# A diffusion layer on one core: the channel mixer in one hand-written order, its down projection in pairs of rows

## The chip, the cores and the metric

The kernel runs on one core of one Trainium2 chip. The metric is device time in microseconds (us) of one execution. The core has five engines that run side by side and wait for each other by semaphores: TensorE (PE; its weight loads are shown as PEld), VectorE (DVE), ScalarE (ACT), GpSimd (POOL) and SyncE (SP), whose queue issues all the data transfers (DMA) of this kernel. Matrix products are written to the eight banks of PSUM; everything else lies in SBUF. Before the change three runs took 1354.81 to 1363.58 us, with a median of 1354.82.

## The reference

One layer of a diffusion backbone: a mixer of mLSTM and attention heads, then a channel mixer, on 1024 latent tokens (and 256 context tokens, which end before the channel mixer), D_MODEL = 1024, D_FF = 2816. Only the channel mixer and the final norm matter here:

```python
def conv_glu(h, w_up, conv_w, conv_b, w_down):
    a, val = jnp.split(h @ w_up, 2, axis=-1)
    a = jax.nn.gelu(dwconv(a, conv_w, conv_b))   # depthwise, width 3, over tokens
    return (a * val) @ w_down
# x = x + gate * conv_glu(modulate(rmsnorm(x, norm_ffn)), ...);  out = rmsnorm(x, final_norm)
```

`h` is 1024 x 1024, `w_up` 1024 x 5632, `w_down` 2816 x 1024, all float32.

## The kernel before, in words

**Products.** Operands are split into a high and a low part (`wh` and `wl`, `hi` and `lo`): ScalarE copies the number to fp32r (a CAST), VectorE subtracts that from the number, and TensorE multiplies high x high, high x low and low x high. A product of one 128-wide weight tile with 512 columns over 4 steps of depth is `prod`: 12 matmuls. Both projections use a scheme in the manner of Strassen and Winograd: seven products of half-size blocks instead of eight, at the price of sums of weights and of results.

**Up projection.** There are 22 blocks, each of 128 gate channels and 128 value channels; they come in the order 0, 11, 1, 12 and so on (`blocks`), as the halves of the rows of `w_down` need them in pairs. The transposed activations `hB` hold seven sums B11, B21, B22 and T1 to T4. For one block the weights (1 MB, four quarters) are loaded into `R` (`load_R`), a tile of seven slots with one buffer. Three slots are sums (`load_up`: two by VectorE, two by GpSimd, one of them in place), and four `wsplit` cut it into `wh` and `wl`: three of 1024 columns, one of 512. The seven products of a block (`upm`) have these names below:

- a = W0[0] x B11, and A = W0[1] x B21, added into the same bank;
- b = W1[1] x T2; c = W1[0] x T1; e = W2[1] x T3; d = W2[0] x T4;
- C = W3 x B22, added into the bank of c.

`sn` is ScalarE's copy of a, made before A. VectorE forms u2 = b + sn, u3 = e + u2, `av` (its second half = c + u3, its first half = d + u3), and after C the value `vt` = c + u2. Then come Identity on ScalarE (`tt` = w av + bias), two taps of the convolution on VectorE, Gelu on ScalarE, the product with a + A on VectorE and that with `vt` on GpSimd. `store` and `combine` put the result, and in every second block its sums with the block before (s1, s2, s4 by GpSimd), into `act_d` in memory; `tt` has two buffers. Block 0 is written out by hand ahead of the loop, up to `fence.__exit__`; behind it only SP's order is written by hand (`sp_order`), and for the other engines a planner decides the order.

**Down projection.** There are seven products m1, m6, m2, m7, m5, m4, m3 of a 512 x 1408 by a 1408 x 512 half each, with 11 rows (`kt`) of 128 each. A step is one row: `load` fetches the row of weights (256 KB) and of activations (256 KB), `cut` splits both, `dprod` does 12 matmuls, 3 into each of the four banks X or Y. `load` runs 6 steps ahead (AHEAD), and steps 1 to 4 are prepared before the last `store` and `combine`. While m1 and m6 run, `sums` makes b22 = b22 - b12 (GpSimd) and b11 = b22 + b11 (VectorE), which m6, m7 and m4 use. Behind each product `after` holds its epilogue for the four tiles, one at a time; behind m4 and m3 stands the final norm (`end2`, `end1`). The last 5 rows (TAIL) of m3 are done tile by tile, so that the norm of one tile runs beside the products of the next.

Of the kernel before, what the change touches and what calls it, by code (L numbers as in the profile page):

```python
# [8 lines left out]
F32 = mybir.dt.float32  # L9
# [8 lines left out]
P = 128  # L18
# [35 lines left out]
DB = 6  # L54
RB = 6
TAIL = 5
AHEAD = 6
# [16 lines left out]
def build(tc, I, out, dbg=None):  # L74
# [1281 lines left out]

    def load_R(m):
        R = fr.tile([P, 7, 512], F32, name="R", tag="R")
        nc.sync.dma_start(R[:, 0:4], I["w_up"][m].rearrange("p q k f -> p q (k f)"))
        return R  # L1360

    def wsplit(R, i, w, eng=V):
        wt = [fw.tile([P, w, 512], F32R, name=f"w{n}{w}", tag=f"w{n}{w}", bufs=5 if w == 2 else 2) for n in "hl"]
        S.copy(wt[0][:], R[:, i:i + w])  # L1364
        sub(eng, wt[1][:], R[:, i:i + w], wt[0][:].bitcast(F32))
        return wt

    def load_up(R):
        add(V, R[:, 4], R[:, 3], R[:, 2])
        sub(V, R[:, 5], R[:, 4], R[:, 0])  # L1370
        sub(G, R[:, 3], R[:, 0], R[:, 3])
        sub(G, R[:, 6], R[:, 1], R[:, 5])
        return [wsplit(R, 0, 2), wsplit(R, 4, 2), wsplit(R, 2, 2), wsplit(R, 6, 1)]
# [3 lines left out]
    add(G, R[:, 4], R[:, 3], R[:, 2])  # L1377
    sub(G, R[:, 5], R[:, 4], R[:, 0])
    sub(G, R[:, 6], R[:, 1], R[:, 5])
# [4 lines left out]
    wB = wsplit(R, 6, 1, V)  # L1384
# [3 lines left out]
    wS = wsplit(R, 4, 2, G)  # L1388
# [14 lines left out]
    sub(G, R[:, 3], R[:, 0], R[:, 3])  # L1403
    sum34(7)
    sum34(4)
    wA = wsplit(R, 2, 2, V)
# [4 lines left out]
    fence.__exit__(None, None, None)  # L1411
# [3 lines left out]

    def upm(m, W, before):
        w = lambda i: spc("ffc", 4 * m + i)
        h1, h2_ = slice(0, 512), slice(512, 1024)
        u2 = fs.tile([P, 512], F32, name="u2", tag="u2")
        u3 = fs.tile([P, 512], F32, name="u3", tag="u3", bufs=1)  # L1420
        av = fs.tile([P, SEQ], F32, name="av", tag="av", bufs=1)
        vt = fs.tile([P, 512], F32, name="vt", tag="vt", bufs=1)
        tt = fs.tile([P, SEQ], F32, name="tt", tag="tt")
        if m == 0:
            a, (c_, b_, f_, e_, d_) = ar0, (ps0[n] for n in "cbfed")
            u2b = fs.tile([P, 512], F32, name="u2b", tag="u2")
            add(V, u2[:], b_[:], ar0[:])
            add(V, ar0[:], ps_a2[:], ar0[:])
            add(V, u2b[:], f_[:], u2[:])
            add(V, u3[:], e_[:], u2[:])  # L1430
            add(V, av[:, h2_], c_[:], u3[:])
            add(V, av[:, h1], d_[:], u3[:])
            add(V, vt[:], c_[:], u2b[:])
        else:
            sn = fs.tile([P, 512], F32, name="sn", tag="sn")
            a = newp(pA, "pa", "a")
            prod(a, W[0], 0, B11, True, True)
            S.copy(sn[:], a[:])
            c_, b_ = newp(pB, "pc", "b"), newp(pB, "pb", "b")
            prod(b_, W[1], 1, T2, True, True)  # L1440
            add(V, u2[:], b_[:], sn[:])
            prod(c_, W[1], 0, T1, True, True)
            e_ = newp(pB, "pe", "b")
            prod(e_, W[2], 1, T3, True, True)
            add(V, u3[:], e_[:], u2[:])
            add(V, av[:, h2_], c_[:], u3[:])
            prod(a, W[0], 1, B21, False, True)
            d_ = newp(pB, "pd", "b")
            prod(d_, W[2], 0, T4, True, True)
            add(V, av[:, h1], d_[:], u3[:])  # L1450
            prod(c_, W[3], 0, B22, False, True)
            add(V, vt[:], c_[:], u2[:])
# [19 lines left out]
        def combine():  # L1472
            if m < KD:
                return
# [292 lines left out]
```

## Time and profile before

| | us |
|---|---|
| three runs: median (lowest, highest) | 1354.82 (1354.81, 1363.58) |
| profiled execution, its own time | 1360.57 |
| its span | 1358.6 |
| block 0 from its first product on | 686.6 to 716.9 |
| block 1 and the last product before block 2 | 716.9 to 743.7 |
| blocks 2 to 21 | 743.7 to 1135.85 |
| down projection | 1135.85 to 1350.4 |
| tail behind the last product | 1350.4 to 1358.6 |

A line of the profile's groups names the source line, engine, operation, and output<-input by the program's names, then shapes, a count, busy time and mean. In brackets stands how long the engine stood idle before, and what ended that. A line of the time order begins with the start in us from the span's start and the duration; a trailing x2 says that two like it follow each other at once. Most splits and sums share a helper's line (L1190, L1355, L1173, L1174), so they are told apart by their tiles. `SPq` rows are issues of transfers.

### The profile page before, as it was taken

The page shows a single profiled execution, that of the slowest core. Times are in us where ns is not written, and L with a number is a line of the kernel's source. Part 1 is how long each engine was busy: PE and PEld are TensorE (multiplying, and loading weights), DVE is VectorE, ACT ScalarE, POOL GpSimd, SP SyncE. Part 2 cuts the span into 40 slices and gives each one's busy share as a digit, 9 for nine tenths or more (in the row PEclk, how much of TensorE's full clock was granted, in tenths as well). Part 3 has the DMA queues.
Part 4 walks back from the last instruction along what each step waited for, and adds up shares of the span by engine and source line. Part 5 has one row for each costly group of instructions (what it writes and reads, how often), then busy time and mean ns, then how long its engine had stood idle before and what let it go on. Part 6 is the DMA issues. An engine that isn't in the chain of part 4 may idle for free.

```text
span 1358.6 us, 20088 instructions
## 1 busy us (share of the span) xinstructions
PE 1281.5 (94%) x7141; PEld 1084.9 (80%) x7141; DVE 980.0 (72%) x1806; ACT 619.3 (46%) x1262; POOL 502.1 (37%) x484
## 2 busy tenths in 40 slices
PE   5999999999898899999978999999999999999997
PEld 4789898999898777778756887778778777787886
DVE  5654787776774788997798666676667675879696
ACT  7532243344464576776754232233323232544454
POOL 0440131313446133332443544454544432455430
PEclk9899899999999899999998999999999999999999
DMA  9431443340025422121422233323332335894745
GB/s 361 158 105 32 141 143 121 107 135 5 19 79 177 156 70 94 63 83 44 157 100 83 76 110 109 100 74 115 116 98 88 117 109 186 269 334 123 250 155 186
DMA packets 83395, 171.43 MB, mean 126 GB/s; under 512 B 12864, under 2 KB 25312, under 8 KB 80480
## 3 DMA queue, kind: packets, MB, share of 16 engines
q1 hardware_dynamic: 83296, 170.16, 38.2%
q8 instruction: 56, 0.92, 0.3%
q14 instruction: 43, 0.35, 0.1%
HBM read 131.84 MB, written 38.29 MB: 125 GB/s over the span
## 4 chain that ended last, share of the span: by engine, by line
DVE 26%; PE 18%; DMA 11%; issue 5%; ACT 5%; POOL 2%; SPq 0%; DVEq 0%; ACTq 0%; POOLq 0%
DMA R<-in_w_up_dram 8%; PE pd L1643 7%; DVE wl L1190 7%; PE u L1070 2%; DVE tt L1454 2%; DVE tt L1455 2%; PE po L298 2%; DVE al L1174 2%; PE po L300 1%; PE po L299 1%; ACT tt L1457 1%; DMA ar<-act_a 1%; DVE nm L1018 1%; DVE dl L1174 1%; DVE hB L1190 1%
## 5 line engine op out<-in xcount | busy, mean ns | idle before, releaser
L1364 ACT CAST wh<-R 128x1024 fp32r<-128x1024 f32 (+1 forms) x87 | 81.4, 940 | 188.6 <-DMA R<-in_w_up_dram 147.2
L1190 POOL TENSOR_TENSOR R<-R 128x512 f32<-128x512 f32 x45 | 86.9, 1939 | 128.1 <-DVE R L1355 127.3
L1190 DVE TENSOR_TENSOR wl<-R,wh 128x1024 fp32r<-128x1024 f32 (+1 forms) x86 | 124.6, 1470 | 5.1 <-ACT wh L1364 5.1
L1283 PE MATMUL pc<-hB,wh 128*128 128x512 f32 x344 | 110.8, 403 | 12.8 <-DVE av L1355 10.8
L1643 PE MATMUL pd<-dh,ah 128*128 128x512 f32 x300 | 116.8, 390 | 1.4 <-ACT ah L1173 1.4
L1643 PE MATMUL pd<-dl,ah 128*128 128x512 f32 x300 | 116.8, 390 | 0.8 <-DVE dl L1174 0.7
L1643 PE MATMUL pd<-dh,al 128*128 128x512 f32 x300 | 116.9, 390 | 0.5 <-DVE al L1174 0.3
L1283 PE MATMUL pa<-hB,wh 128*128 128x512 f32 x336 | 103.8, 389 | 0.0
L1283 PEld LDWEIGHTS pc<-hB,wh 128*128 128x128 f32 x344 | 64.6, 192 | 32.4 <-DVE av L1355 17.0
L1174 DVE TENSOR_TENSOR al<-ar,ah 128x512 fp32r<-128x512 f32 x76 | 71.2, 938 | 19.9 <-ACT ah L1173 19.6
L1355 DVE TENSOR_TENSOR R<-R 128x512 f32<-128x512 f32 x21 | 14.5, 691 | 90.8 <-DMA R<-in_w_up_dram 90.8
L537 PE MATMUL pp<-hl,wh 128*128 128x512 f32 x256 | 79.8, 403 | 0.0
L660 POOL TENSOR_SCALAR dm<-ident,mh 128x128 fp32r<-128x128 f32 x64 | 27.5, 431 | 137.3 <-PE pe L667 96.7
L1173 ACT CAST ah<-ar 128x512 fp32r<-128x512 f32 x76 | 47.1, 620 | 65.1 <-DMA ar<-act_s 33.8
L298 PE MATMUL pv<-wh,hl 128*128 128x256 f32 x256 | 75.7, 296 | 0.0
L1283 PEld LDWEIGHTS pa<-hB,wh 128*128 128x128 f32 x336 | 63.2, 188 | 13.2
L299 PE MATMUL pv<-wl,hl 128*128 128x256 f32 x256 | 73.1, 285 | 0.0
L300 PE MATMUL pv<-wh,hl 128*128 128x256 f32 x256 | 72.9, 285 | 0.0
L1459 POOL TENSOR_TENSOR tt<-vt,tt 128x512 f32<-128x512 f32 x22 | 29.9, 1360 | 111.7 <-ACT tt L1457 74.2
L1283 PE MATMUL pc<-hB,wl 128*128 128x512 f32 x172 | 68.5, 398 | 0.0
L1643 PEld LDWEIGHTS pd<-dh,ah 128*128 128x128 f32 x300 | 56.3, 188 | 13.9 <-ACT ah L1173 2.3
L1643 PEld LDWEIGHTS pd<-dl,ah 128*128 128x128 f32 x300 | 56.3, 188 | 13.4 <-DVE dl L1174 1.7
(1060 smaller groups left out, 4028.0 us busy)
## 6 DMA issues: line engine op xcount, KB each, us to landing
R<-in_w_up_dram SPq DMA_DIRECT2D x22, 1024.0 KB, 6.1
w<-in_w_ada_dram SPq DMA_DIRECT2D x64, 256.0 KB, 2.8
br<-in_w_down_dram SPq DMA_DIRECT2D x55, 256.0 KB, 4.5
ar<-act_s SPq DMA_DIRECT2D x44, 256.0 KB, 3.8
act_a<-tt SPq DMA_DIRECT2D x33, 256.0 KB, 6.7
act_s<-tt SPq DMA_DIRECT2D x33, 256.0 KB, 6.4
ar<-act_a SPq DMA_DIRECT2D x33, 256.0 KB, 4.5
wr<-in_w_h_dram SPq DMA_DIRECT2D x16, 512.0 KB, 5.0
```

The source lines that it names most:

```text
L298: T.matmul(ps, st_hi, mv_hi, start=first, stop=False)
L299: T.matmul(ps, st_hi, mv_lo, start=False, stop=False)
L300: T.matmul(ps, st_lo, mv_hi, start=False, stop=last)
L537: T.matmul(pp[:, 512 * n:512 * n + 512], wkq[sw][:, kt, cs], hl[n][part][:, kt, :], start=kt == 0 and sw + part == 0, stop=kt == KT - 1 an ...
L660: G.tensor_scalar(out=dm[:, d], in0=ident[:], scalar1=mhf[:, d, c, h:h + 1], scalar2=1.0, op0=ALU.mult, op1=ALU.mult)
L1173: S.copy(hi, src)
L1174: V.tensor_tensor(out=lo, in0=src, in1=hi.bitcast(F32), op=ALU.subtract)
L1190: sub = lambda e, o, x, y: e.tensor_tensor(out=o, in0=x, in1=y, op=ALU.subtract)
L1283: T.matmul(ps[:], wt[sw][:, j, ks], hB[part][:, blk, kt, :], start=first and kt == 0 and sw + part == 0, stop=last and kt == 3 and sw == 1 ...
L1364: S.copy(wt[0][:], R[:, i:i + w])
L1459: G.tensor_tensor(out=tt[:, h2_], in0=vt[:], in1=tt[:, h2_], op=ALU.mult)
L1643: T.matmul(ps[:], ac[sa][:, js], w[sw], start=first and n == 0, stop=last and n == 2, skip_group_check=not fresh)
```

## The change

The up projection is now a class `Block` with one method for each piece of work, and one loop calls them in a hand-written order that holds on all engines (`fence` is left only at the very end of the kernel, behind the last output). The products of a block are in the order a, b, A, c, e, d, C; before they were a, b, c, e, A, d, C. The work of block i-1 behind its last product (vt, taps, Gelu, the two products, combine) stands among the products of block i. `R` becomes two tiles: `Ra` with the first two quarters, and `Rb` with the other two and the three sums, each with one buffer and a load of its own (512 KB). The first split of the next block needs only `Ra`; the sums are made at the end of the iteration before.

In the down projection a step is a pair of rows (the last a single one): one load of weights for two rows, casts and splits of 1024 columns, 24 matmuls. `load` runs 4 pairs ahead and `cut` two. Rows 0 to 7 of m1 are prepared ahead (before: 0 to 5). The subtraction for m5 goes from GpSimd to VectorE. Part of the epilogue of m5 and m4 goes from VectorE to GpSimd, and the last norms follow a list (`plan`).

The core of the diff:

```diff
     def load_R(m):
-        R = fr.tile([P, 7, 512], F32, name="R", tag="R")
-        nc.sync.dma_start(R[:, 0:4], I["w_up"][m].rearrange("p q k f -> p q (k f)"))
+        R = fr.tile([P, 2, 512], F32, name="Ra", tag="Ra"), fr.tile([P, 5, 512], F32, name="Rb", tag="Rb")
+        for t in range(2):
+            nc.sync.dma_start(R[t][:, 0:2], I["w_up"][m, :, 2 * t:2 * t + 2].rearrange("p q k f -> p q (k f)"))
         return R
...
+    W = {0: wsplit(R, 0)}
+    sums(R)
+    for n in range(1, 4):
+        W[n] = wsplit(R, n)
+    R = load_R(blocks[2])
+    for i in range(1, NF):
...
+        C.pe("a")
+        if i > 1:
+            split_w(0)
+        C.sn_()
+        if i == 1:
+            B.av2()
+            B.av1()
+            B.ident_()
+        B.vt_()
+        B.taps()
+        if i < 3:
+            sums(R)
+        if i == 1:
+            split_w(0)
+        C.pe("b")
+        B.gelu()
+        B.mul1()
+        B.mul2()
+        C.u2_()
+        split_w(1)
+        C.pe("A")
+        C.pe("c")
+        split_w(2, 3)
+        if i < NF - 2:
+            R = load_R(blocks[i + 2])
...
+        B.combine()
...
+        C.pe("e")
+        C.pe("d")
+        C.av2()
...
+        C.av1()
+        C.ident_()
+        if 1 < i < NF - 2:
+            sums(R)
+        C.pe("C")
+        B = C
```

```diff
-DB = 6
-RB = 6
-TAIL = 5
-AHEAD = 6
+DB = 2
+RB = 4
+AHEAD = 4
...
+    raws.update({1: (b11[1], early[1]), 2: (b11[2], early[2]), 3: (b11[3], [a[:].unsqueeze(1) for a in (a6, a7)])})
+    cut(1)
+    C.ident_()
+    C.vt_()
+    C.taps()
+    cut(2)
+    C.gelu()
+    C.mul1()
+    C.mul2()
+    C.combine()
...
-    sums = {1 + k * 8 // 5: k for k in range(KD)}
+    sums = {(2, 3, 4, 6, 7, 8)[j]: j for j in range(NP)}
...
+            if n + 2 in raws:
+                q, k = steps[n + 2]
+                m = len(PAIRS[k])
+                W_ = raws[n + 2][0]
+                if q == "m5":
+                    W_ = W_[:, 0:m]
+                    sub(V, W_, W_, more.pop(n + 2)[:, 0:m])
+                cut(n + 2)
+                if q == "m2":
+                    sub(G, b11[k][:, 0:m], b11[k][:, 0:m], W_[:, 0:m])
...
+            plan = [todo[1:3], part(size2, 4, 5) + todo[3:4], part(size2, 6) + part(end2, 4, 5) + todo[4:5],
+                    part(size2, 7) + part(end2, 6) + part(after_m3, 0), part(end2, 7) + part(after_m3, 1) + part(end1, 0),
+                    part(after_m3, 2) + part(end1, 1), part(after_m3, 3) + part(end1, 2, 3)]
```

VectorE's order in one block of the up projection, from the sums of the weights (`R<-R`, later `Rb<-Rb`) on; `wl` is a split, `u` with `pb` is u2, `tt` with `sp` a tap. Before:

```order
L1355 TENSOR_TENSOR R<-R 128x512
L1190 TENSOR_TENSOR R<-R 128x512
L1355 TENSOR_TENSOR av<-pd,u_10949 128x512
L1190 TENSOR_TENSOR wl_11060<-R,wh_11059 128x1024
L1190 TENSOR_TENSOR wl_11064<-R,wh_11063 128x1024
L1355 TENSOR_TENSOR vt<-pc,u_10948 128x512
L1454 SCALAR_TENSOR_TENSOR tt<-av,sp,tt 128x1023
L1190 TENSOR_TENSOR wl_11072<-R,wh_11071 128x512
L1455 SCALAR_TENSOR_TENSOR tt<-av,sp,tt 128x1023
L1458 TENSOR_TENSOR tt<-pa,tt 128x512
L1355 TENSOR_TENSOR u_11081<-pb,sn 128x512
L1190 TENSOR_TENSOR wl_11068<-R,wh_11067 128x1024
```

And now the same place (`av` with `pd` stands just ahead of the first row):

```order
L1354 TENSOR_TENSOR Rb<-Rb 128x512
L1189 TENSOR_TENSOR Rb<-Rb,Ra 128x512
L1189 TENSOR_TENSOR wl_8915<-Ra,wh_8914 128x1024
L1354 TENSOR_TENSOR vt<-pc,u_8801 128x512
L1472 SCALAR_TENSOR_TENSOR tt<-av,sp,tt 128x1023
L1474 SCALAR_TENSOR_TENSOR tt<-av,sp,tt 128x1023
L1481 TENSOR_TENSOR tt<-pa,tt 128x512
L1354 TENSOR_TENSOR u_8940<-pb,sn 128x512
L1189 TENSOR_TENSOR wl_8945<-Rb,wh_8944 128x1024
L1189 TENSOR_TENSOR wl_8974<-Rb,wh_8973 128x1024
L1189 TENSOR_TENSOR wl_8978<-Rb,wh_8977 128x512
L1354 TENSOR_TENSOR u_8941<-pe,u_8940 128x512
```

`av` of d moved ahead of the sums, and two of the three splits of `Rb` that stood among the taps moved behind u2.

SP's order at the start of the down projection, from the stores of the last block (`act_a`, `act_s` as outputs) on; `b_6` is a row of weights of m1, `b_0` with `br` a row for `sums`, `ar` activations. Before:

```order
L1461 DMA act_s_10_160<-tt 128x512
L1534 DMA b_6_11526<-in_w_down_dram 128x512
L1536 DMA ar<-act_a_6_90 128x512
L1657 DMA b_0_11531<-in_w_down_dram 128x512
L1659 DMA br<-in_w_down_dram 128x512
L1657 DMA b_1_11532<-in_w_down_dram 128x512
L1659 DMA br<-in_w_down_dram 128x512
L1534 DMA b_7_11527<-in_w_down_dram 128x512
L1536 DMA ar<-act_a_7_91 128x512
L1534 DMA b_8_11528<-in_w_down_dram 128x512
```

And now (`b_4` is rows 8 and 9 of m1):

```order
L1488 DMA act_s_10_160<-tt 128x512
L1601 DMA b_4_11558<-in_w_down_dram 128x2x512
L1605 DMA ar<-act_a_8_92 128x512
L1605 DMA ar<-act_a_9_93 128x512
L1601 DMA b_0_11560<-in_w_down_dram 128x2x512
L1601 DMA br<-in_w_down_dram 128x2x512
L1601 DMA b_5_11559<-in_w_down_dram 128x512
L1605 DMA ar<-act_a_10_94 128x512
L1601 DMA b_1_11561<-in_w_down_dram 128x2x512
L1601 DMA br<-in_w_down_dram 128x2x512
```

The first load behind the stores served row 6 of m1; it now serves rows 8 and 9.

401 lines of the change are left out of this document (225 added, 176 removed).

## The prediction

> **What bounds the kernel now.** I read the page's busy times first, then busy time by stage (columns: stretch in us, its length, busy time and instructions of each engine, granted clock, DMA share, GB/s), then who the TensorE waits for, then the engines' rows around those waits.
>
> ```profile
> span 1358.6 us, 20088 instructions
> PE 1281.5 (94%) x7141; PEld 1084.9 (80%) x7141; DVE 980.0 (72%) x1806; ACT 619.3 (46%) x1262; POOL 502.1 (37%) x484
> 686.60:716.90 30.30, 23.62 (x96) 17.06 (x95) 27.91 (x38) 15.47 (x31) 16.36 (x10) 0.94 0.18 66
> 716.90:743.70 26.80, 22.01 (x86) 17.38 (x85) 22.24 (x21) 11.28 (x12) 9.95 (x6) 0.88 0.28 88
> 743.70:1135.85 392.15, 384.89 (x1681) 314.11 (x1680) 261.18 (x276) 126.56 (x140) 177.97 (x98) 1.00 0.33 102
> 1135.85:1350.40 214.55, 211.80 (x925) 172.77 (x923) 173.81 (x221) 102.92 (x187) 87.84 (x57) 1.00 0.65 220
> 1350.40:1358.60 8.20, 0.02 (x1) 0.00 (x0) 2.96 (x5) 2.46 (x5) 0.00 (x0) 0.79 0.55 204
> 752.00 0.62 PE L1283 MATMUL pe<-hB,wh 128*128 128x512 f32 x2
> 754.72 0.62 PE L1283 MATMUL pa<-hB,wh 128*128 128x512 f32 x2
> ```
>
> The mixer is the last half of the span and TensorE is its bound. The number of products is fixed, so the change can win only the time in which TensorE stands. The last two rows give the unhindered pace: one product (12 matmuls) takes 754.72 - 752.00 = 2.72 us, one block of seven 19.04 us, one matmul 0.2267 us. So blocks 2 to 21 need 20 x 19.04 = 380.8 of their 392.15 us: 11.35 us are lost. The down projection needs 924 x 0.2267 = 209.45 of its 214.55: 5.1 lost. Blocks 0 and 1 (716.90 to 743.70 and the stretch before) lose more; 8.2 us of tail follow.
>
> ```profile
> PE pc L1283 <- DVE av L1355: 7.3, 10, 0.9
> 896.70 0.33 SPq L1359 DMA_DIRECT2D R<-in_w_up_dram  x1
> 903.39 3.99 POOL L1190 TENSOR_TENSOR R<-R 128x512 f32<-128x512 f32 x2 [5.63 <-DVE R L1355]
> 904.50 3.96 DVE L1190 TENSOR_TENSOR wl<-R,wh 128x1024 fp32r<-128x1024 f32 x2
> 914.45 1.22 DVE L1190 TENSOR_TENSOR wl<-R,wh 128x1024 fp32r<-128x1024 f32 x1
> 915.74 0.33 SPq L1359 DMA_DIRECT2D R<-in_w_up_dram  x1
> 922.04 0.69 DVE L1355 TENSOR_TENSOR R<-R 128x512 f32<-128x512 f32 x1 [5.04 <-DMA R<-in_w_up_dram]
> 923.38 0.68 DVE L1355 TENSOR_TENSOR av<-pd,u 128x512 f32<-128x512 f32 x1
> 935.71 0.33 SPq L1359 DMA_DIRECT2D R<-in_w_up_dram  x1
> ```
>
> TensorE's waits (total, times, longest) in blocks 2 to 21 name one place: the last product C, which adds into the bank that VectorE's `av` still has to read. Behind it is a loop: `R` has one buffer, its load is issued when the block's last split ends (914.45 + 1.22 = 915.67, issue 915.74), VectorE stands 5 us until it lands, then works through sums, `av`, splits and taps up to the next last split. From issue to issue over two blocks this takes 935.71 - 896.70 = 39.01 us, against 2 x 19.04 = 38.08 for TensorE. VectorE's loop, not TensorE, sets the pace, by about 1 us in two blocks.
>
> **The change, part by part.** *Steady blocks.* Removed from the loop: half of the load's length, because `Ra` (read early) and `Rb` are now two tiles and two loads and only `Rb` waits for the last split; and `av` of d, which now stands in front of the sums, in the time of the load. For 512 KB the same tensor has one row, another weight a second:
>
> ```profile
> R<-in_w_up_dram SPq DMA_DIRECT2D x22, 1024.0 KB, 6.1
> er<-in_w_up_dram SPq DMA_DIRECT2D x1, 512.0 KB, 3.7
> wr<-in_w_h_dram SPq DMA_DIRECT2D x16, 512.0 KB, 5.0
> act_s<-tt SPq DMA_DIRECT2D x33, 256.0 KB, 6.4
> 922.10 1.05 ACT L1364 CAST wh<-R 128x1024 fp32r<-128x1024 f32 x1 [7.94 <-DMA R<-in_w_up_dram]
> 1117.23 1.24 ACT L1453 ACTIVATE tt<-av,sp 128x1024 f32<-128x1024 f32 x1 [6.17 <-DMA act_s<-tt]
> ```
>
> I take 3.7 (same tensor, same queue), a gain of 2.4 a block; 5.0 (1.1) is the other end. `av` gives 0.6 a block. Added: ScalarE's copy for a block's first split now stands behind Identity of the block in work, and in every second block Identity writes the `tt` buffer that the stores s1 and s2 read (the last row shows such a wait); these stores are queued on SP behind the load's issue. s2 is issued some 1.7 us after `Rb`; it lands between 1.7 + 4.0 (6.4 less the half load no longer ahead of it) and 1.7 + 6.4 us; I take 7.3, near the upper end, because the other stores stay ahead of it. Then Identity (1.24), the copy of the first split (1.05) and only then the first split: it starts 9.6 us after the issue, where load and sums alone would allow 3.7 + 1.4 = 5.1: 4.5 us, less 0.7 because GpSimd's two subtractions then run in VectorE's idle time. Sum for two blocks: 39.0 - 2 x 2.4 - 2 x 0.6 + 4.5 - 0.7 = 36.8, under 38.08. So TensorE sets the pace again, and C is not late: e ends only one product (d, 2.72 us) ahead of C, where it was two, but VectorE has the splits behind it by then (the last one ends some 12.3 to 13.5 us into the block, e at 13.6, C is due at 16.3) and needs 0.68 + 0.69 for u3 and `av`. Gain 11.35 us. With both upper ends it is 39.0 - 2.2 - 1.2 + 4.5 = 40.1, and nothing is gained. A moved from behind e to before c costs nothing: it needs ScalarE's `sn`, done one product earlier. Sums on VectorE, halves for the splits and combine keep their operations.
>
> *Blocks 0 and 1.* The rows up to `u2b` stay. Now all four splits of block 1 go ahead of block 0's `av`.
>
> ```profile
> 713.29 0.68 DVE L1355 TENSOR_TENSOR u2b<-pf,u 128x512 f32<-128x512 f32 x1
> 718.73 0.50 PE L1283 MATMUL pb<-hB,wh 128*128 128x512 f32 x1 [1.26 <-ACT wh L1364]
> 731.24 6.75 DVE L1190 TENSOR_TENSOR wl<-R,wh 128x1024 fp32r<-128x1024 f32 x4
> 737.91 0.68 DVE L1355 TENSOR_TENSOR av<-pc,u 128x512 f32<-128x512 f32 x1
> 734.73 0.39 PE L1283 MATMUL pa<-hB,wh 128*128 128x512 f32 x1
> 738.65 1.22 PE L1283 MATMUL pc<-hB,wh 128*128 128x512 f32 x2 [3.53 <-DVE av L1355]
> 743.93 0.50 PE L1283 MATMUL pa<-hB,wh 128*128 128x512 f32 x1
> 738.00:743.90 5.90, 5.25 (x12) 4.12 (x13) 2.47 (x3) 1.24 (x1) 0.00 (x0) 0.50 0.82 230
> ```
>
> The wait of 1.26 us at the start of block 1 goes, since `Ra` lands early and its split stands first; it only lengthens the next wait. C(1) still needs `av`, and VectorE's list up to there has the same work: after 713.97 thirteen 512-wide operations at 0.61 from start to start, two taps at 1.2, six 1024-wide splits (three at 1.2, three beside GpSimd at 6.75 less a 512-wide one, over three: 2.0), 2 us of waits for copies: 7.9 + 2.4 + 9.6 + 2 = 21.9, so `av` ends near 737 instead of 738.6. TensorE is through with d(1) at 716.9 + 6 x 2.72 = 733.2 and stands 4 us. Behind the 3.5 us wait of before its clock was 0.50 and C took 743.93 - 738.65 = 5.28 us instead of 2.72; I keep that price. C(1) ends near 742.7 instead of 743.7: gain 1.0. Bounds: -1 (every split beside GpSimd) and 5.8 (`av` 2 us earlier and full clock).
>
> [...]
>
> *Down projection.* Rows in pairs: the same bytes in half as many weight loads, casts and splits twice as wide (no cost: two 512-wide at 0.6 equal one at 1.2). What stands at its start:
>
> ```profile
> 1143.10 3.71 SPq L1461 DMA_DIRECT2D act_s<-tt  x3
> 1146.91 0.39 SPq L1534 DMA_DIRECT2D b<-in_w_down_dram  x1
> 1152.09 0.62 ACT L1173 CAST dh<-b 128x512 fp32r<-128x512 f32 x1 [7.28 <-DMA b<-in_w_down_dram]
> 1154.06 3.15 POOL L1190 TENSOR_TENSOR b<-b,br 128x512 f32<-128x512 f32 x2 [7.59 <-DMA br<-in_w_down_dram]
> 1150.00:1180.00 30.00, 27.65 (x118) 21.57 (x117) 22.32 (x29) 14.59 (x26) 11.07 (x8) 1.00 0.86 292
> ```
>
> SP is held by the last block's stores until 11.1 us after the end of C(21); the first load behind them serves step 6, due after 6 x 2.72 = 16.3, and came at 16.2 with its cast still to do. Now eight rows are prepared ahead instead of six, so that load is due at 21.8 and lands near 18: that wait goes. What is late next: m6's operands, due after 11 rows at 29.9. VectorE's split for it stands behind the sum of the second pair: 3.5 MB of loads from 12 us on at 292 GB/s (25), GpSimd 3.15 (28.2), sum 1.2, two splits 2.4: 31.8. So 1.9 us are lost there and 0.5 at the next step: 2.4 instead of 5.1, gain 2.7; bounds 5.1 (all covered) and -2 (loads at 250 GB/s). The subtraction of m5 moved from GpSimd to VectorE (six of 1.2 us) is covered: m5's step of 5.44 us holds 2.4 of splits, 1.2 and 0.7. In m4 GpSimd gets eight more operations, off any path that TensorE waits on.
>
> *Tail.*
>
> ```profile
> 1350.03 0.39 PE L1643 MATMUL pd<-dh,al 128*128 128x512 f32 x1
> 1351.08 0.68 DVE L1586 TENSOR_TENSOR tm<-pd,gfr 128x512 f32<-128x512 f32 x1
> 1353.81 0.72 ACT L1600 ACTIVATE o<-o,rn 128x512 f32<-128x512 f32 x1 [0.23 <-DVE rn L1598]
> ```
>
> The last multiply no longer waits behind another tile's scaling (1351.08 instead of 1350.5: gain 0.55), but the last copy stands behind that tile's copy (0.7) and two more stores. Zero, within 0.5.
>
> Sum: 11.35 + 1.0 + 2.7 + 0 = 15.05 us. The profiled execution took 1360.57 us (span 1358.6 and 2.0 around it), 5.75 over the median of 1354.82; I take the gain from the median: 1339.8, rounded 1340 (a profiled one near 1345.6).
>
> **The rivals.** (1) VectorE's loop stays the bound. For it: GpSimd's sums and combine now fall together with VectorE's splits, and two 1024-wide splits beside GpSimd took 3.96 us (904.50), a single one elsewhere 1.22. If every split meets GpSimd, each pair costs about 2 us more than summed: 38.8, a loss of 0.7 x 10 = 7 us: 1347. [...] (2) The other side: Identity waits for the stores s1 and s2 and the loop gets longer than before. It decides from 39.2 us for two blocks on; at the upper ends, 40.1, all of the 11.35 goes and 9 us come on top, with the other gains kept: 1354.8 + 9 - 3.7 = 1360; slower by over 1% would need 41 us. Against it: the stores are issued as soon as `Rb` is. [...] (4) The order does nothing that TensorE feels in the up projection, because C still waits for VectorE and only later: 11.35 and 1.0 are not won, 2.7 is: 1352. For it: e, which `av` needs, ends later in the block than it did. Against it: the wait in blocks 2 to 21 was at most 0.9, and the loop has 1.3 us less in two blocks than TensorE needs.
>
> **How the numbers follow.** The forecast has 0.60, with 1336 to 1345 as its own range; rival 1 has 0.15 (1344 to 1351), rival 2 0.07, rival 3 0.12, rival 4 0.06. The range of 1334 to 1350 leaves out rivals 2 and 4 and the ends. The bound of 1% (about what a measurement of this kernel can tell from no change) lies at 1341.3, inside the forecast's range: faster 0.70 x 0.60 + 0.12 + 0.1 x 0.15 = 0.56; slower 0.05 (rival 2 from 41 us on, and what I do not see); same 0.39.
>
> **What would show it.** Right: loads of `Rb` 19.04 us apart on average, no wait of C for `av` from block 3 on, one wait of C in block 1 with the clock at 0.50 behind it, 380.8 to 382 us for blocks 2 to 21, and in the down projection one short wait at m6's start. Wrong: C waiting for `av` in every second block with Identity waiting for the stores (rival 2) or with splits of 2 us throughout (rival 1), waits inside m1, or a stop of VectorE behind GpSimd in m4 or m7.

## The result, and the profile after

The changed kernel takes 1367.46 us (median of 22 runs, 1359.68 to 1380.23), the kernel before 1356.21 (22 runs of the same session, 1349.92 to 1368.46): a ratio of 1.0081, 95% interval 1.0058 to 1.0104. That is 0.8% or 11 us slower, inside the 1% bound, and on the other side of the forecast of 15 us faster. (The ratio leaves out one run of the changed kernel, which fell in a slower state.) The profiled execution of the changed kernel took 1370.23 us; its span is 1368.4.

Busy time by stage, in the columns used in the prediction; the stages are cut at the mixer's first product, a(1), a(2), the end of C(21) and the last product. The changed kernel:

```profile
684.48:719.34 34.86, 26.19 (x95) 19.21 (x94) 27.22 (x37) 16.01 (x32) 16.11 (x10) 0.85 0.18 62
719.34:745.78 26.44, 20.91 (x86) 16.88 (x84) 22.56 (x21) 11.82 (x13) 9.47 (x6) 0.87 0.32 100
745.78:1141.74 395.96, 387.44 (x1682) 313.53 (x1680) 280.23 (x278) 124.57 (x141) 168.99 (x98) 1.00 0.32 103
1141.74:1361.00 219.26, 212.94 (x925) 173.98 (x923) 171.24 (x148) 90.31 (x118) 88.78 (x44) 0.99 0.63 213
```

The kernel before, cut in the same way (the prediction has nearly the same cuts), has 30.25, 26.84, 392.15 and 214.57 us. Three stages got longer: the first stretch by 4.6 us, blocks 2 to 21 by 3.8, the down projection by 4.7; block 1 is 0.4 shorter and the tail (7.39 instead of 8.18) 0.8. Together 11.9 us from the mixer's first product on, about the 11.25 between the medians. (That product itself starts anywhere from 676 to 689 us in the profiles of this study, so below stage lengths are compared, not spans.) One number stands out: in blocks 2 to 21 VectorE is busy for 280.2 us instead of 261.2, with 278 instructions instead of 276.

**First stretch.** Rows in order of time of the changed kernel, and then of the kernel before, around the load for block 0:

```profile
680.46 0.42 SPq L1360 DMA_DIRECT2D Ra<-in_w_up_dram  x1
685.63 0.32 SPq L1333 DMA_DIRECT2D x_d<-x  x1
686.00 1.76 SPq L1360 DMA_DIRECT2D Rb<-in_w_up_dram  x1
691.41 1.29 POOL L1354 TENSOR_TENSOR Rb<-Rb 128x512 f32<-128x512 f32 x1 [12.50 <-DMA Rb<-in_w_up_dram]
695.41 0.62 ACT L1377 CAST wh<-Rb 128x512 fp32r<-128x512 f32 x1 [5.30 <-POOL Rb L1189]
```

```profile
683.28 0.33 SPq L1359 DMA_DIRECT2D R<-in_w_up_dram  x1
687.75 0.32 SPq L1334 DMA_DIRECT2D x_d<-x  x1
688.41 1.65 POOL L1355 TENSOR_TENSOR R<-R 128x512 f32<-128x512 f32 x1 [7.38 <-DMA R<-in_w_up_dram]
```

The one load of before stood on SP ahead of the store of the last x tile. Of the two loads only `Ra` stands there; `Rb` is queued behind the store, which waits for x until 685.6, and GpSimd's sums, ScalarE's copy and the first products that need them are late by that.

**Blocks 2 to 21.** Two blocks of the changed kernel, from one load of `Rb` to the second next:

```profile
919.15 0.33 SPq L1360 DMA_DIRECT2D Rb<-in_w_up_dram  x1
919.54 0.90 SPq L1488 DMA_DIRECT2D act_a<-tt  x2
920.49 6.12 SPq L1488 DMA_DIRECT2D act_s<-tt  x3
923.69 0.69 DVE L1354 TENSOR_TENSOR Rb<-Rb 128x512 f32<-128x512 f32 x1 [2.49 <-DMA Rb<-in_w_up_dram]
924.49 1.77 POOL L1189 TENSOR_TENSOR tt<-tt 128x512 f32<-128x512 f32 x1 [5.91 <-DVE Rb L1354]
926.33 1.24 ACT L1464 ACTIVATE tt<-av,sp 128x1024 f32<-128x1024 f32 x1 [11.19 <-POOL tt L1189]
928.55 1.29 DVE L1189 TENSOR_TENSOR wl<-Ra,wh 128x1024 fp32r<-128x1024 f32 x1 [3.44 <-ACT wh L1377]
935.35 4.11 DVE L1189 TENSOR_TENSOR wl<-Rb,wh 128x1024 fp32r<-128x1024 f32 x3
939.49 0.33 SPq L1360 DMA_DIRECT2D Rb<-in_w_up_dram  x1
941.42 1.25 ACT L1464 ACTIVATE tt<-av,sp 128x1024 f32<-128x1024 f32 x1 [4.89 <-DVE av L1354]
944.28 0.69 DVE L1354 TENSOR_TENSOR Rb<-Rb 128x512 f32<-128x512 f32 x1 [2.90 <-DMA Rb<-in_w_up_dram]
945.62 2.32 DVE L1189 TENSOR_TENSOR wl<-Ra,wh 128x1024 fp32r<-128x1024 f32 x1
953.88 5.15 DVE L1189 TENSOR_TENSOR wl<-Rb,wh 128x1024 fp32r<-128x1024 f32 x3
959.06 0.33 SPq L1360 DMA_DIRECT2D Rb<-in_w_up_dram  x1
```

39.9 us, where the forecast had 36.8 and TensorE needs 38.08. In the first of the two blocks Identity starts 7.2 us after the issue of `Rb`, in the second 1.9. In the first it has to wait until the readers of its `tt` buffer are done: the stores s1 and s2, and GpSimd's subtraction for s4 (924.49), itself behind a store of the same group; all of these stores stand on SP behind the load of `Rb`. In four of the nine pairs whose Identity waits, the store lands last, and once much later (Identity starts 9.4 us after the issue); then `sn`, which follows Identity on ScalarE, keeps A waiting too. That is the longest of A's five waits:

```profile
886.71 1.24 ACT L1464 ACTIVATE tt<-av,sp 128x1024 f32<-128x1024 f32 x1 [13.42 <-DMA act_s<-tt]
889.42 0.74 PE L1282 MATMUL pa<-hB,wh 128*128 128x512 f32 x2 [2.33 <-ACT sn L1448]
```

**Down projection.** TensorE's four waits there, with what VectorE did ahead of them:

```profile
1154.73 0.43 SPq L1601 DMA_DIRECT2D b<-in_w_down_dram  x1
1166.05 1.23 DVE L1354 TENSOR_TENSOR er<-b,er 128x1024 f32<-128x1024 f32 x1 [2.88 <-POOL b L1189]
1167.19 0.69 DVE L1173 TENSOR_TENSOR dl<-b,dh 128x512 fp32r<-128x512 f32 x1
1167.79 2.88 DVE L1173 TENSOR_TENSOR al<-ar,ah 128x512 fp32r<-128x512 f32 x1
1170.73 0.50 PE L1752 MATMUL pd<-dh,al 128*128 128x512 f32 x1 [1.18 <-DVE al L1173]
1172.87 3.38 DVE L1173 TENSOR_TENSOR al<-ar,ah 128x1024 fp32r<-128x1024 f32 x1
1176.31 0.50 PE L1752 MATMUL pd<-dh,al 128*128 128x512 f32 x1 [2.52 <-DVE al L1173]
...
1246.77 0.68 DVE L1692 TENSOR_TENSOR tm<-pd,gfr 128x512 f32<-128x512 f32 x1
1249.39 0.15 DVE L1698 TENSOR_SCALAR rn<-rn 128x1 f32<-128x1 f32 x1 [0.85 <-ACT jk L1696]
1250.34 1.48 DVE L1173 TENSOR_TENSOR dl<-b,dh 128x1024 fp32r<-128x1024 f32 x1 [0.79 <-ACT dh L1172]
1251.74 2.31 DVE L1173 TENSOR_TENSOR al<-ar,ah 128x1024 fp32r<-128x1024 f32 x1
1253.97 0.68 DVE L1692 TENSOR_TENSOR tm<-pd,gfr 128x512 f32<-128x512 f32 x1
1267.28 0.49 PE L1752 MATMUL pd<-dh,ah 128*128 128x512 f32 x1 [0.81 <-ACT ah L1172]
1269.82 0.50 PE L1752 MATMUL pd<-dh,al 128*128 128x512 f32 x1 [1.71 <-DVE al L1173]
```

The first two waits are m1's last row and m6's first: the first load behind the stores comes 13.0 us after C(21) (11.1 before), and the split of m1's last row (1167.19) stands behind the sum for m6 (1166.05), which waits 2.88 us for GpSimd. The splits that TensorE then waits for run beside GpSimd's subtractions (1167.71, 2.42 us, and 1171.75, 3.42 us) and take 2.88 us instead of 0.69 and 3.38 instead of 1.22: 2.2 us more each. The late loads bear on the first wait alone: in e7, where the first load comes 9.1 us after C(21), m1's last row does not wait, and m6's first row waits the same 2.52 us.

The last two waits are m5's first row. Ahead of it, in m7, one step takes VectorE 1253.97 - 1246.77 = 7.2 us and TensorE 5.44: VectorE waits for ScalarE's square of a tile (0.85) and then for the copy that stands behind that square (0.79), and so falls behind by 1.8 us a step. In the same step the splits and a sum beside GpSimd take 1.7 us more than elsewhere (1.48 and 2.31 instead of 1.22, and 1.07 instead of 0.69).

### The profile page after: what moved, and what is told of

It reads as the page before. It is cut to its first block, busy times and chain, and to the rows that moved or that the text cites. A ratio compares the mean times of both kernels' runs of the same rounds, so it can differ in the third digit from the quotient of the medians.

```text
span 1368.4 us, 19850 instructions
## 1 busy us (share of the span) xinstructions
PE 1285.2 (94%) x7141; PEld 1085.3 (79%) x7141; DVE 998.1 (73%) x1736; ACT 605.7 (44%) x1195; POOL 492.9 (36%) x471
## 4 chain that ended last, share of the span: by engine, by line
PE 27%; DVE 19%; DMA 7%; issue 7%; ACT 5%; POOL 1%; SPq 1%; ACTq 0%; DVEq 0%; POOLq 0%
PE pd L1752 9%; DVE wl L1189 4%; DMA Rb<-in_w_up_dram 3%; DMA act_s<-tt 3%; PE pa L1282 2%; PE pc L1282 2%; PE u L1069 2%; DVE tt L1472 2%; DVE tt L1474 2%; PE po L297 2%; PE pb L1282 2%; PE po L299 1%; PE po L298 1%; DVE al L1173 1%; ACT tt L1478 1%
## 5 line engine op out<-in xcount | busy, mean ns | idle before, releaser
L1189 POOL TENSOR_TENSOR Rb<-Ra,Rb 128x512 f32<-128x512 f32 x44 | 71.7, 1649 | 92.4 <-DVE Rb L1354 92.3
L1189 DVE TENSOR_TENSOR wl<-Rb,wh 128x1024 fp32r<-128x1024 f32 (+1 forms) x65 | 100.0, 1587 | 6.7 <-ACT wh L1377 6.7
L1464 ACT ACTIVATE tt<-av,sp 128x1024 f32<-128x1024 f32 x22 | 27.4, 1245 | 165.5 <-DVE av L1354 62.7
L1752 PEld LDWEIGHTS pd<-dh,al 128*128 128x128 f32 x296 | 55.9, 189 | 18.8 <-DVE al L1173 7.4
L1173 DVE TENSOR_TENSOR al<-ar,ah 128x1024 fp32r<-128x1024 f32 (+1 forms) x37 | 66.0, 1783 | 0.1
L1282 PE MATMUL pa<-hB,wl 128*128 128x512 f32 x168 | 65.4, 389 | 0.0
```

Source lines behind the costliest of these rows:

```text
L1173: V.tensor_tensor(out=lo, in0=src, in1=hi.bitcast(F32), op=ALU.subtract)
L1189: sub = lambda e, o, x, y: e.tensor_tensor(out=o, in0=x, in1=y, op=ALU.subtract)
L1282: T.matmul(ps[:], wt[sw][:, j, ks], hB[part][:, blk, kt, :], start=first and kt == 0 and sw + part == 0, stop=last and kt == 3 and sw == 1 ...
L1464: S.activation(self.tt[:], self.av[:], AF.Identity, bias=self.w(3), scale=self.w(1))
L1752: T.matmul(ps[:], ac[sa][:, js], w[sw], start=first and n == 0, stop=last and n == 2, skip_group_check=not fresh)
```

## The experiments

Stage lengths in us, and the ratio of time to the kernel before, which ran in each session beside them:

| | first stretch | block 1 | blocks 2-21 | down | from first product on | ratio (95%) |
|---|---|---|---|---|---|---|
| before | 30.25 | 26.84 | 392.15 | 214.57 | 671.99 | 1 |
| after | 34.86 | 26.44 | 395.96 | 219.26 | 683.92 | 1.0081 (1.0058, 1.0104) |
| e1 | 30.73 | 27.47 | 397.55 | 218.78 | 681.94 | 1.0067 (1.0043, 1.0090) |
| e2 | 34.42 | 27.13 | 387.86 | 221.94 | 678.72 | 1.0060 (1.0031, 1.0089) |
| e3 | 34.96 | 26.30 | 397.17 | 218.84 | 684.68 | 1.0090 (1.0067, 1.0113) |
| e4 | 30.58 | 28.67 | 428.49 | 220.78 | 716.48 | 1.0324 (1.0278, 1.0370) |
| e5 | 34.13 | 27.28 | 383.30 | 221.57 | 673.69 | 0.9972 (0.9943, 1.0001) |
| e6 | 34.65 | 27.37 | 396.60 | 216.26 | 682.33 | 1.0058 (1.0033, 1.0082) |
| e7 | 34.56 | 25.44 | 380.81 | 217.24 | 665.46 | not compared |
| e8 | 30.63 | 27.33 | 382.14 | 217.03 | 664.56 | 0.9923 (0.9897, 0.9948) |
| e9 | 30.44 | 27.36 | 382.42 | 214.79 | 662.39 | 0.9936 (0.9913, 0.9958) |
| e10 | 30.65 | 27.42 | 382.98 | 214.30 | 662.80 | 0.9945 (0.9919, 0.9972) |
| e11 | 30.71 | 28.57 | 382.53 | 213.49 | 662.71 | 0.9948 (0.9919, 0.9977) |

**e1: the load ahead of the store.**

```diff
-    R = load_R(0)
+    with tc.high_priority():
+        R = load_R(0)
```

> Edit: on SP the load of Rb for block 0 stands ahead of the store of the last x tile, not behind it; nothing else moves. Theory (SP's queue): the 4.6 us that the stretch from the mixer's first product to a(1) lost (34.9 us instead of 30.25) are this one transfer, issued at 686.0 though its room was free earlier. Then Rb is issued near 681 to 682, GpSimd's first sum starts near 687, the waits of pf and pb go, and the stretch takes 30 to 31 us: 4 to 4.6 us off the whole. Rival (room: the memory of Rb is freed only by the last products of the stage before): the issue stays at 685 or later and the stretch stays within 1 us of 34.9. Rival (GpSimd's three sums are late for another reason, such as x's own store beside them): Rb lands early and pf still waits.

Measured: `Rb` is issued 0.7 us behind `Ra`, and the first stretch takes 30.73 us:

```profile
676.46:707.19 30.73, 23.63 (x95) 17.41 (x94) 28.10 (x37) 15.95 (x32) 16.00 (x10) 0.94 0.19 72
```

The 4.1 us are SP's queue; both rivals fall. Part of it is lost again within the same run: block 1 and blocks 2 to 21 are 2.6 us longer together. Why is open; e6, which changes nothing up to there, has 1.6 us of it too, so most of it may be the spread between executions.

**e2: Identity behind the next split's copy and `sn`.**

```diff
         C.sn_()
+        if i > 1:
+            B.ident_()
...
         C.av1()
-        C.ident_()
```

> Edit: on ScalarE, Identity of a block stands behind the copy of the next block's first split and behind sn, instead of ahead of both. Theory (Identity waits for the stores s1 and s2, and the first split waits behind it): every second block's first split starts about 5.9 instead of 9.4 us after the issue of Rb, and then runs beside GpSimd's sums (2.3 instead of 1.25 us): two blocks take 39.8 - 3.5 + 1.1 = 37.4 us by VectorE, below TensorE's 38.08, so blocks 2 to 21 take 381 to 385 instead of 396 us, C waits 0.2 us at most, and A does not wait for sn: 11 to 15 us off the whole. Rival (the splits beside GpSimd set the pace, the wait is hidden): two blocks stay at 39 us or more, blocks 2 to 21 at 391 or more. Rival (order of the products, e only one product ahead of C): C goes on waiting 0.55 us in every second block and the rest of the waits goes: 390.

Measured: the first split starts 5.8 us after the issue of `Rb` in nearly every block and takes 2.3 us; two blocks take 38.5 us, blocks 2 to 21 387.86. That is 8 us off, not 11 to 15: Identity now waits for `sn`, thus for a, at 7.6 us in both kinds of block, and the chain from there to `av` and C is as long as TensorE's block (C starts within 0.1 us of the end of `av` in every block but the last). In the down projection 2.7 us are lost: the first load behind the stores comes 16.1 us after C(21), TensorE's waits grow by 1.1 us, and the other 1.6 lie outside its waits. The direction is that of the theory, the size was not.

**e3: the old order of the products.**

```diff
-        C.pe("A")
         C.pe("c")
...
         C.pe("e")
+        C.pe("A")
         C.pe("d")
```

> Edit: the products of a block in the order of before, a b c e A d C, in the loop of the changed kernel; nothing else moves. Theory (VectorE's loop sets the pace, at 39.8 us for two blocks, and only where TensorE notices it depends on the order): blocks 2 to 21 stay at 394 to 397 us; A's waits for sn go, those of C grow or move to e. Rival (the new order of the products is what costs: e, which av needs, ends one product ahead of C instead of two): C's waits go and blocks 2 to 21 take 382 to 388 us.

Measured: 397.17, the same; A's waits are gone and C's are longer (up to 3.0 us). The order of the products, the first thing that the change names, neither costs nor wins anything as long as VectorE's loop sets the pace.

**e4: one load per block.**

```diff
-        R = fr.tile([P, 2, 512], F32, name="Ra", tag="Ra"), fr.tile([P, 5, 512], F32, name="Rb", tag="Rb")
...
+        R = fr.tile([P, 7, 512], F32, name="R", tag="R")
+        nc.sync.dma_start(R[:, 0:4], I["w_up"][m].rearrange("p q k f -> p q (k f)"))
+        return R[:, 0:2], R[:, 2:7]
```

> Edit: R is one tile again with one load of 1024 KB per block, in the order of the changed kernel. Theory (the half load shortens VectorE's loop, by less than I took): the sums start 6.1 us instead of 4.55 behind the issue, the block whose Identity does not wait takes 1.6 us longer, the other one, which waits for Identity, none: 41.4 us for two blocks and 408 to 412 us for blocks 2 to 21, 12 to 16 us more; the first stretch of the mixer takes 30 to 31 us, since this load stood ahead of the store of x in the kernel before, which gives back 4. Rival (the load is hidden anyway, because Identity is the later one everywhere): blocks 2 to 21 stay at 396. Rival (the two half loads cost more than one): they take less than 394.

Measured: 428.49, 32.5 us more than with two loads, twice what the theory had. The block whose Identity does not wait is 1.5 us longer, as expected; the other one too, by 2.0, since the stores stand behind the longer load and Identity starts 9.2 us behind the issue instead of 7.25. The issue rows of the page, of the changed kernel and then of e4:

```profile
act_s<-tt SPq DMA_DIRECT2D x33, 256.0 KB, 5.1
```

```profile
act_s<-tt SPq DMA_DIRECT2D x33, 256.0 KB, 6.6
```

In this order the split of `R` is worth more than was forecast for it. The kernel before, with one load and two buffers of `tt` as well, takes 392.15 us, so in its order the one load was affordable; what the split would be worth there was not run. The first stretch goes back to 30.58.

**e5: three buffers of `tt`.**

```diff
-            self.tt = fs.tile([P, SEQ], F32, name="tt", tag="tt")
+            self.tt = fs.tile([P, SEQ], F32, name="tt", tag="tt", bufs=3)
...
```

> Edit: tt has three buffers instead of two (room for it comes from one buffer each for sn and u2 instead of two, and u2b lies in s3's place); the order of every engine stays. Theory (Identity of every second block waits for the stores s1 and s2, which read the buffer it writes): Identity starts 1.9 to 2 us after the issue of Rb in every block, the first split at 5.9, two blocks take VectorE 19.3 + 18.3 = 37.6 us, below 38.08, and blocks 2 to 21 take 381 to 385 instead of 396 us, with no wait of A for sn. The down projection stays at 218 to 220 (the order of its start is not touched). Rival (the order on ScalarE alone was the cost, not the buffer): Identity still starts late in every second block. Rival (contention with GpSimd then takes the place of the wait): two blocks stay above 38.6 us, 387 or more.

Measured: 383.30 us for blocks 2 to 21. Identity starts as soon as `av` is there, and A does not wait. One buffer takes 12.7 us away here. VectorE's loop is not the 37.6 us of the theory, though: loads of `Rb` are mostly 38.3 to 38.8 us apart over two blocks, still above TensorE's 38.08, so VectorE lives on its lead from block 1, which lasts about half of the loop. From there on C starts right behind `av` in most blocks and is up to 0.3 us late, which is the 2.5 us that remain over 380.8. VectorE's busy time even rises:

```profile
739.62:1122.92 383.30, 383.09 (x1681) 314.46 (x1680) 299.47 (x278) 125.64 (x141) 185.63 (x98) 1.00 0.33 106
```

The down projection takes 221.57 us instead of the 218 to 220 expected. Its waits are those of the changed kernel to 0.1 us; behind them the clock is lower (0.72 from 1157.5 to 1161.0, where the changed kernel has 1.00 at the same place), which is 3.5 x 0.28 = 1.0 us of the 2.3 between the two. So lengths of this stage carry about 2 us that the order does not decide.

**e6: two places in the down projection.**

```diff
+    vsums = {(3, 4, 5, 6, 7, 8)[j]: j for j in range(NP)}
...
-            if n in sums:
-                k = sums[n]
+            if n in vsums:
+                k = vsums[n]
...
     def after_m2(i):
-        scaled(V, tmp_()[:], X[i][:], i, 0)
-        norm1(i, 0)
-        scaled(G, tmp_()[:], us[i][:], i, 1)
+        if i:
+            norm1(i - 1, 0)
+        if i < 4:
+            scaled(V, tmp_()[:], X[i][:], i, 0)
+            scaled(G, tmp_()[:], us[i][:], i, 1)
```

> Two edits in the down projection: VectorE's sum for m6's first pair stands behind the split of m1's last row, not ahead of it (and the next two sums accordingly); and in the epilogue of m2, which runs beside m7, ScalarE's square of a tile and what follows it stand one step later, behind the next step's copies and splits. Theory: of the 10.3 us that the down projection takes over 924 x 0.2267 = 209.45 (219.27 with the last product's length), the waits at m1's last row and m6's first (1.34 + 2.68) go down to 1.5 or less, and those at m5's first row (0.97 + 1.97, and 1.3 of half clock) go: 212 to 214.5 instead of 219.3. Rival (loads, not VectorE's order, are late there: the first load after the stores comes 13.0 us behind C(21)): the first two waits stay and only m5's go: 215. Rival (m5's waits come from GpSimd beside VectorE in m7): those stay and the others go: 216.

Measured: half of it. The waits at m5 are gone altogether, so taking the square out of the way is enough; splits beside GpSimd in m7 take 2.2 and 2.3 us in this run too, so these alone do not make m5 wait. At m1's last row the wait is gone and at m6's first row 0.63 us are left; the stall moved to m6's second pair (1.89 and 0.64 us, with the clock at 0.56 from 1186.2 to 1190.0 behind them): its sum now stands behind a split, runs beside GpSimd (3.41 us instead of 1.2), and its copy and split follow one after the other.

```profile
1176.18 3.30 POOL L1189 TENSOR_TENSOR b<-b,br 128x1024 f32<-128x1024 f32 x1 [1.17 <-DMA br<-in_w_down_dram]
1177.15 3.41 DVE L1354 TENSOR_TENSOR b<-b,b 128x1024 f32<-128x1024 f32 x1
1185.11 0.49 PE L1754 MATMUL pd<-dl,ah 128*128 128x512 f32 x1 [1.89 <-DVE dl L1173]
```

**e7: without GpSimd's sums of results.**

```diff
-                sub(G, s3[:], tt[:, h1], tt[:, h2_])
...
-            add(G, p[:, h2_], p[:, h2_], tt[:, h2_])
...
-            sub(G, p[:, h1], p[:, h2_], p[:, h1])
...
-            sub(G, tt[:, h1], tt[:, h1], p[:, h1])
```

> GpSimd's subtractions and sums for s1, s2, s3 and s4 are left out in the up projection; the stores stay and write the uncombined halves. It measures what GpSimd's work beside VectorE's splits costs. Theory (both count: waiting for the stores 2.4 us of two blocks, GpSimd beside the three splits behind u2 3.2 us): the three splits take 3.0 us in every block instead of 4.11 and 5.15, Identity of every second block still starts 6 us or more after the issue of Rb, two blocks take at most 37.5 us by VectorE, and blocks 2 to 21 take 381 to 385. Rival (splits are slow for another reason, ScalarE's copies beside them): they stay at 4.1 and 5.1 and blocks 2 to 21 above 390.

Measured (the kernel leaves out part of the layer's work, so its time is not set beside the others): the three splits behind u2 take 2.96 to 3.05 us, Identity of every second block still starts 7.2 us after the issue, and blocks 2 to 21 take TensorE's own 380.81:

```profile
749.44:1130.25 380.81, 380.81 (x1681) 315.32 (x1680) 242.71 (x278) 127.07 (x141) 92.87 (x58) 1.00 0.33 107
```

With 40 operations less on GpSimd VectorE is busy 280.2 - 242.7 = 37.5 us less for the same 278 instructions: each of them costs VectorE about 0.94 us on average. Against e5, which has the same 40 operations and no late Identity, it is (299.5 - 242.7) / 40 = 1.42 us, so the price depends on what they meet. The loop of the changed kernel is too long by two things: without GpSimd's sums it is within TensorE's pace, and without the late Identity it is so nearly within it that 2.5 us are left over 20 blocks.

**e8: all remedies together**, and in the last block the taps ahead of `vt` and of the splits of rows 2 to 5.

```diff
-    cut(1)
     C.ident_()
-    C.vt_()
     C.taps()
-    cut(2)
+    C.vt_()
+    cut(1)
     C.gelu()
     C.mul1()
     C.mul2()
     C.combine()
+    cut(2)
```

> All edits together: Rb of block 0 ahead of the store of x, three buffers of tt, the two new places in the down projection, and in the last block the taps ahead of vt and of the splits of rows 2 to 5, so that its stores and the loads behind them come earlier. Theory (the three losses are separate and add up): first stretch 30.5, block 1 26.5 to 27.5, blocks 2 to 21 381 to 385, down 211 to 214, tail 7.4: 657 to 665 us from the mixer's first product on, where the kernel before takes 672 and the changed one 684: faster than before by 0.5 to 1.1%, about 1340 to 1349 at the usual median. Rival (what is won in one stage is given back in the next, as the earlier start of the down projection meets the same stores and loads): 668 to 674, no difference from before.

Measured: 0.9923 of before, and three of the stages as expected; the down projection takes 217.03 instead of 211 to 214. In its rows the stall at m6's second pair is the one of e6.

**e9 and e10: the sums for m6.** e9 takes the first edit of e6 back (`sums` instead of `vsums`); e10 keeps it and moves GpSimd's third subtraction:

```diff
-    sums = {(2, 3, 4, 6, 7, 8)[j]: j for j in range(NP)}
+    sums = {(2, 3, 5, 6, 7, 8)[j]: j for j in range(NP)}
```

> As the run with all edits, but VectorE's sums for m6 stand again where the changed kernel has them (ahead of the split of m1's last row). Theory (the sum moved back made a chain of sum, ScalarE's copy and split for every pair, so the stall only moved from m6's first pair to its second): the waits at m6's second pair (2.16 + 0.9 and 1.4 of half clock) go; as the last block's stores and the loads behind them now come 2 us earlier, m1's last row and m6's first row wait 2 us or less together: down 211 to 214 instead of 217.0. Rival (the loads, not the order of the sums, set the start): the waits come back at m1's last row and m6's first as 3 to 4 us, down 215 to 218. Other stages as in that run.

> As the run with all edits, but GpSimd's subtraction for the third pair (and its two loads) comes one step later. Theory (the second pair of m6 was late because VectorE's sum for it took 3.41 us beside that subtraction, instead of 1.2): that sum takes 1.2 to 1.3 us, m6's second pair is ready 2.1 us earlier, its waits (2.16 + 0.9) shrink to 0 to 1 and the clock stays up: down 212 to 214. Rival (the loads it needs then come later and the third pair waits instead): down stays at 216 to 218.

Measured: 214.79 and 214.30. In e9 the second pair is in time and one wait is left, at m6's first row, of 2.57 us, with the clock at 0.51 from 1155.2 to 1158.4 behind it; m1's last row waits 0.14 us; the loads begin 0.9 us earlier (12.1 us after C(21)). In e10 the sum for the second pair takes 1.21 us, as expected, but a split of the same pair meets GpSimd's next subtraction instead (3.41 us), and the pair waits 2.08 us. Both runs are a little above what was expected (at most 214 in both), with one stall of 2 to 2.6 us left at m6, behind a split of 3.4 us beside GpSimd in both. By time e8, e9 and e10 can't be told apart.

**e11: two pieces of VectorE's list in block 1 to GpSimd**, on top of e9.

```diff
-        W[n] = wsplit(R, n)
+        W[n] = wsplit(R, n, G if n == 2 else V)
...
-            sums(R)
+            sums(R, G if i == 1 else V)
```

> As e9_sums_as_changed, and in block 1 two pieces of VectorE's list go to GpSimd, which stands idle there: the split for e and d of block 1, and the two sums for block 2. Theory (VectorE's list up to av of block 1 is what C(1) waits for, 5.76 us): the list is 2.5 to 3.5 us shorter, C(1) waits 2.3 to 3.3 us, and with the shorter stall the clock falls for less or not at all, so that the five to ten products from a(1) to a(2) take 22 to 24.8 us instead of 27.3. Rival (GpSimd is slower there and its sums come late: the splits of block 2 wait for them): the stretch stays at 26.5 to 28 us. Blocks 2 to 21 stay at 381 to 384.

Measured: neither the theory nor the rival's 26.5 to 28. C(1) waits 7.25 us instead of 5.77, and the stretch takes 28.57. The first fence is e9, the second e11, VectorE's and TensorE's rows up to C(1):

```profile
712.14 4.10 DVE L1189 TENSOR_TENSOR wl<-Rb,wh 128x1024 fp32r<-128x1024 f32 x3 [1.12 <-ACT wh L1377]
720.80 1.28 DVE L1475 SCALAR_TENSOR_TENSOR tt<-av,sp,tt 128x1023 f32<-128x1023 f32 x1
727.88 4.51 DVE L1189 TENSOR_TENSOR wl<-Rb,wh 128x1024 fp32r<-128x1024 f32 x3
733.77 1.22 PE L1282 MATMUL pc<-hB,wh 128*128 128x512 f32 x2 [5.77 <-DVE av L1354]
```

```profile
707.71 5.17 DVE L1189 TENSOR_TENSOR wl<-Rb,wh 128x1024 fp32r<-128x1024 f32 x2 [1.12 <-ACT wh L1377]
717.43 2.19 DVE L1475 SCALAR_TENSOR_TENSOR tt<-av,sp,tt 128x1023 f32<-128x1023 f32 x1
724.09 5.56 DVE L1189 TENSOR_TENSOR wl<-Rb,wh 128x1024 fp32r<-128x1024 f32 x3
731.03 1.22 PE L1282 MATMUL pc<-hB,wh 128*128 128x512 f32 x2 [7.25 <-DVE av L1354]
```

VectorE's list has fewer instructions and gets longer: two splits take 5.17 us beside GpSimd's one, where three took 4.10, and a tap takes 2.19 instead of 1.28.

## Why the prediction was wrong

**Steady blocks: +3.8 instead of -11.35.** The step that failed is the sum of VectorE's loop for two blocks, 36.8, against about 39.8 measured (most pairs are 20.4 + 19.4). Its mechanism was right almost to the digit: the first split behind a waiting Identity was to start 9.6 us after the issue and starts 9.4 (928.55 - 919.15), though in five of the nine pairs it is GpSimd's subtraction for s4 that ends last, which the forecast did not name. Three terms were mis-sized:

- *The half load.* 3.7 us was taken from the one row of the same tensor, a load that stood alone; `Rb` lands in 4.5 in the loop, and the sums start 4.6 us after the issue on average, where they started 6.2: 1.6 us gained in a block, not 2.4. Error 1.6 for two blocks.
- *The late Identity.* 4.5 us were charged; with the load longer it is 9.4 - 5.9 = 3.5. Error -1.0.
- *The splits.* They were kept at their old prices, less 0.7. In the kernel before two blocks had 2 x (3.96 + 0.68 + 1.22) = 11.7 us of them (904.50 and 914.45 in the prediction, and the 512-wide one beside them); now 1.29 + 4.11 + 2.32 + 5.15 = 12.9, as the hand-written order puts three of the four behind u2, beside GpSimd's combine. Nearly all of the difference is the 512-wide one, 1.77 instead of 0.68 in every second block. Error 1.9.

36.8 + 1.6 - 1.0 + 1.9 = 39.3; the remaining 0.5 I do not assign. So rival 1 (splits beside GpSimd) and rival 2 (Identity behind the stores) both came true at once. Each had been priced alone, on top of a loop with 1.3 us to spare; their sum was no case of its own, though 39.2 had been named as the point from which it decides. e5 and e7 show that it takes both to lose 15 us: without either one the stage takes 383.3 or 380.8. Rival 4's reason, e ending later, falls with e3.

**Blocks 0 and 1: +4.2 instead of -1.0.** "The rows up to u2b stay" is the step that failed. On the compute engines it holds; on SP it does not, because one load became two and the second stands behind a store (e1). The forecast had gone through the queue's order for the loop and for the last block, and not for the load that is issued ahead of both. In block 1 VectorE's list up to `av` was summed as 21.9 us and takes 25.2 (716.13 to 741.30), with splits of 2.3 us and the product with a + A (1.78 instead of 0.61) beside GpSimd. The recorded sum also has a slip: 713.97 + 21.9 is 735.9, not near 737, which would have left a wait of 2.7 us. The wait of C was to be 4 us and is 5.5, with the clock at 0.50 from 741.3 to 744.5 behind it as forecast (C takes 4.4 us instead of 2.72). Rival 3 (0.12, at 1335) and the upper bound of 5.8 with its full clock take it that the clock stays up behind a stall about 2 us shorter. No run shows that term: the wait of C grew, and in the down projection the clock behind a wait of 2.52 us was 1.00, behind one of 2.57 us (e9) 0.51, and behind two of 0.81 and 1.71 us 0.58 (1269.8 to 1273.5).

**Down projection: +4.7 instead of -2.7.** Where 2.4 us were to be lost at the start of m6, TensorE waits 2.5 there and 1.2 at m1's last row. The place was right, and the chain too up to VectorE: GpSimd's second subtraction ends 28.4 us after C(21), 28.2 in the forecast. The step that failed is "two splits 2.4": beside GpSimd's third subtraction they take 1.21 + 3.38. The split of m1's last row had been passed over; it stands behind a sum and runs beside GpSimd too. The loads begin 13.0 us after C(21) and not 11.1; with the taps ahead of the splits they begin at 12.1 (e8), so VectorE's list ahead of Gelu is part of that, and the rest is not shown. "The subtraction of m5 is covered" fails outright: the cover was looked for in m5's own step, but m5's first row is prepared in m7, where VectorE has no slack when each step waits for ScalarE twice (e6: with the square a step later m5 does not wait). That wait is neither in the sum nor a rival; the prediction spoke of VectorE behind GpSimd in m7, and the wait that decides was ScalarE's.

**Tail: -0.8** instead of 0, a little outside the 0.5 that was given.

## What to carry to other kernels

When a load or a store is split in two, or an engine's order is written by hand, go through every in-order queue from end to end and ask for each entry what now stands ahead of it, also in the code that the change doesn't seem to touch. A loop that is forecast with 1.3 us to spare in 38 is not safe: price its known delays together, not as rivals one by one, and give each operation the duration it has beside its new neighbours. And before an order is blamed, look for the buffer: here one more `tt` won 12.7 us in the loop, where e2 and e3, which change the order alone, won 8.1 and nothing.

## What the runs showed of the hardware

GpSimd's work beside VectorE is not free for VectorE: 0.94 us on average for each 512-wide operation taken out of the changed kernel, 1.42 us against e5 (both with e7), and in e11 work moved to an idle GpSimd made VectorE's shorter list longer (two splits 5.17 us, where three took 4.10 in e9). Only some rows are touched. In blocks 2 to 21 of the changed kernel `u`, `av` and `vt`, which read a bank of PSUM, keep 0.68 to 0.69 us; u2 has GpSimd at work beside it in all 20 blocks. The split of `Ra`, with both operands in SBUF, takes 1.22 to 1.33 us nine times, with GpSimd idle for most of it, and 2.31 to 2.32 nine times, with GpSimd at work; a sum for m6 takes 3.41 us beside GpSimd's subtraction in e6 and 1.21 in e10. It is not every row with both operands in SBUF: the sum `Rb<-Rb,Ra` keeps 0.69 us, with GpSimd at work for most of it in all 19 blocks that have one.

TensorE's clock does not follow from the length of one stall. The same wait at m6's first row left it at 1.00 in the changed kernel (2.52 us) and at 0.51 for 3.2 us in e9 (2.57 us), the first and second row below; e11, with e9's down projection and a wait of 2.52 us there, kept 1.00 and took 213.49 us for the stage instead of 214.79:

```profile
1176.30:1179.50 3.20, 3.19 (x14) 2.62 (x15) 3.20 (x3) 2.00 (x3) 1.10 (x1) 1.00 0.75 236
```

```profile
1155.20:1158.40 3.20, 3.20 (x8) 2.52 (x9) 3.20 (x3) 2.01 (x3) 1.66 (x1) 0.51 0.81 246
```

Why the clock halved in e9 stays open.
